# Two stores moved behind the last load, and part of the first x loaded in six-partition transfers, in a batched matmul

## The chip, the cores and the metric

The kernel runs on one core of a Trainium2 chip. The metric is the device time of one execution in microseconds (us). Before the change it was 517.46 us (median of 3 runs, 517.2 to 518.03). Faster or slower needs 2%; kernels were measured in up to five rounds beside runs of the kernel before on the same chip (three chips in all, so compare runs of the same rounds first). A ratio below is the mean time of one kernel's fast runs over that of the other's of the same rounds, so it is not quite the ratio of the quoted medians.

## The reference

```python
batch, m, k, n = 32, 512, 1024, 768
x = randn(batch, m, k)            # float32
weight = randn(batch, k, n)       # float32
out = np.matmul(x, weight)        # float32
```

## The kernel before

Every batch loads 2 MB of x and 3 MB of weights from HBM and stores 1.5 MB. All loads but the first x are issued by GpSimd (POOL) on the *software queue*, which casts float32 to bfloat16 on the way (the page counts 1024 KB for such a load of x, half of what it reads). The first x goes as float32 on SyncE's (SP's) *hardware queue* (2048 KB on the page), and so do the stores of the end. TensorE (PE) transposes x and multiplies; ScalarE and VectorE copy the results out of its accumulators. Loads are issued three to four batches ahead. The last four batches take their weights in pieces.

```python
CHUNKED = {B - 4: (4, 4), B - 3: (4, 4), B - 2: (4, 4), B - 1: (4, 2, 2)}
AHEAD = 3
LATE = 4
# w_pool has 4 buffers, x_pool 5, out_pool 7                      (cut)

x_first = first_pool.tile([P, MT, K], F32)            # 128 x 4 x 1024
nc.sync.dma_start(x_first, x_view[0])                 # hardware queue
load_w(0)                                             # software queue
...
for b in range(B):
    if b + AHEAD + 1 < B:
        load_x(b + AHEAD + 1)                         # software queue
    if b + AHEAD < B:
        load_w(b + AHEAD)                             # software queue
    if 0 < b <= B - LATE:
        nc.gpsimd.dma_start(out=out_view[b - 1], in_=outs[b - 1])
    if b == B - 1:                                    # hardware queue
        # half of out[30], out[28], out[29], the other half of out[30]  (cut)
    ...  # transposes, matmuls, evacuation; out[31] goes in two halves on SP
```

Of the kernel before, what the change touches and what calls it, by code (L numbers as in the profile page):

```python
# [12 lines left out]
@with_exitstack  # L13
def kernel(
    ctx: ExitStack,
    tc: tile.TileContext,
    x: bass.AP,
    weight: bass.AP,
    out: bass.AP,
):  # L20
    nc = tc.nc
    B, M, K = x.shape
    _, _, N = weight.shape
    P = 128
    MT = M // P
    KT = K // P
    JT = KT // 2
    N2 = 2 * N
    CHUNKED = {B - 4: (4, 4), B - 3: (4, 4), B - 2: (4, 4), B - 1: (4, 2, 2)}
    AHEAD = 3  # L30
    LATE = 4

    const = ctx.enter_context(tc.tile_pool(name="const", bufs=1))
    first_pool = ctx.enter_context(tc.tile_pool(name="first", bufs=1))
    w_pool = ctx.enter_context(tc.tile_pool(name="w", bufs=4))
    x_pool = ctx.enter_context(tc.tile_pool(name="x", bufs=5))
    xT_pool = ctx.enter_context(tc.tile_pool(name="xT", bufs=8))
    out_pool = ctx.enter_context(tc.tile_pool(name="out", bufs=7))
    tpsum = ctx.enter_context(tc.tile_pool(name="tpsum", bufs=2, space=bass.MemoryType.PSUM))
    mpsum = ctx.enter_context(tc.tile_pool(name="mpsum", bufs=2, space=bass.MemoryType.PSUM))  # L40



    w_view = weight.rearrange("b (ki ko) n -> b ki ko n", ki=P)
    x_view = x.rearrange("b (mi mo) k -> b mi mo k", mi=P)
    out_view = out.rearrange("b (mi mo) n -> b mi (mo n)", mi=P)

    xs, ws, outs = {}, {}, {}

    def banks():  # L50
        return [mpsum.tile([P, 512], F32, name=f"pm{i}") for i in range(3)]

    def load_x(b):
        xs[b] = x_pool.tile([P, MT, K], BF16, name="x_sb")
        nc.gpsimd.dma_start(out=xs[b], in_=x_view[b])  # L55

    def load_w(b):
        ws[b] = w_pool.tile([P, KT, N], BF16, name="w_sb")
        at = 0
        for n in CHUNKED.get(b, (KT,)):  # L60
            nc.gpsimd.dma_start(out=ws[b][:, at:at + n, :], in_=w_view[b, :, at:at + n, :])  # L61
            at += n

    def transpose(b, mt):

        pt = tpsum.tile([P, JT, P], F32, name="pt")
        pairs = xs[b].bitcast(F32)
        for j in range(JT):
            nc.tensor.transpose(pt[:, j, :], pairs[:, mt, j::JT], ident)  # L69
        xT = xT_pool.tile([P, JT, P, 2], BF16, name="xT")  # L70
        nc.vector.tensor_copy(  # L71
            xT.rearrange("p j m r -> p (j m r)"), pt.bitcast(BF16).rearrange("p j m -> p (j m)")
        )
        return xT

    def transpose_first(mt):

        xT = xT_pool.tile([P, JT, P, 2], BF16, name="xT")
        for h in range(2):
            pt = tpsum.tile([P, JT, P], F32, name="pt")  # L80
            for i in range(JT):
                nc.tensor.transpose(pt[:, i, :], x_first[:, mt, JT * h + i::KT], ident)  # L82
            nc.vector.tensor_copy(  # L83
                xT[:, 2 * h:2 * h + 2].rearrange("p j m r -> p j r m"),
                pt.rearrange("p (j r) m -> p j r m", r=2),
            )
        return xT



    SPLITS = (
        ((0, 0, 0, 512), (1, 0, 512, N - 512)),
        ((1, N - 512, 0, 1024 - N), (2, 0, 1024 - N, N2 - 1024)),
    )

    def matmuls(pm, half, xT, b, kos, together):
        for ko in kos:
            for i, (bank, at, off, size) in enumerate(SPLITS[half]):
                shares = half == 1 and i == 0
                nc.tensor.matmul(  # L100
                    pm[bank][:, at:at + size],
                    xT[:, ko // 2, :, ko % 2],
                    ws[b][:, ko, off:off + size],
                    start=(ko == 0 and not (together and shares)),
                    stop=(ko == KT - 1),
                    skip_group_check=together,
                )

    def evacuate(b, pair, pm):
        o = outs[b][:, pair * N2:(pair + 1) * N2]  # L110
        nc.scalar.copy(o[:, 0:512], pm[0])  # L111
        nc.vector.tensor_copy(o[:, 512:1024], pm[1])  # L112
        nc.scalar.copy(o[:, 1024:N2], pm[2])  # L113

    with tc.manual_schedule():
        x_first = first_pool.tile([P, MT, K], F32)
        nc.sync.dma_start(x_first, x_view[0])
        load_w(0)
        ident = const.tile([P, P], F32)
        make_identity(nc, ident)  # L120
        for b in range(1, AHEAD):
            load_x(b)
            load_w(b)
        load_x(AHEAD)

        for b in range(B):
            if b + AHEAD + 1 < B:
                load_x(b + AHEAD + 1)
            if b + AHEAD < B:
                load_w(b + AHEAD)  # L130
            if 0 < b <= B - LATE:
                nc.gpsimd.dma_start(out=out_view[b - 1], in_=outs[b - 1])  # L132
            if b == B - 1:
                halves = [slice(pair * N2, (pair + 1) * N2) for pair in range(2)]
                nc.sync.dma_start(out_view[b - 1, :, halves[0]], outs[b - 1][:, halves[0]])
                for late in range(B - LATE, B - 2):
                    nc.sync.dma_start(out_view[late], outs[late])
                nc.sync.dma_start(out_view[b - 1, :, halves[1]], outs[b - 1][:, halves[1]])
            outs[b] = out_pool.tile([P, MT * N], F32, name="out_sb")
            if b not in CHUNKED:  # L140
                turn = transpose if b else lambda _, mt: transpose_first(mt)
                xT = {mt: turn(b, mt) for mt in (0, 1)}
                for pair in range(2):
                    pm = banks()
                    for half in range(2):
                        if pair == 0:
                            matmuls(pm, half, xT[half], b, range(KT), False)
                            xT[2 + half] = turn(b, 2 + half)
                        else:
                            matmuls(pm, half, xT[2 + half], b, range(KT), False)  # L150
                    evacuate(b, pair, pm)
                continue
            xT = {0: transpose(b, 0)}
            pms = [banks() for _ in range(2)]
            at = 0
            for n in CHUNKED[b]:
                last = at + n == KT
                for mt in range(MT):
                    if mt + 1 not in xT and mt + 1 < MT:
                        xT[mt + 1] = transpose(b, mt + 1)  # L160
                    matmuls(pms[mt // 2], mt % 2, xT[mt], b, range(at, at + n), True)
                    if last and mt % 2 == 1:
                        pair = mt // 2
                        evacuate(b, pair, pms[pair])
                        if b == B - 1:
                            nc.sync.dma_start(out_view[b, :, halves[pair]], outs[b][:, halves[pair]])
                at += n
# [30 lines left out]
```

## Time and profile before

| | before |
|---|---|
| time, median | 517.46 us |
| span of the profiled run | 515.2 us |
| PE busy | 429.3 us (83%) |
| software queue, share of 16 DMA engines | 96.8% |
| HBM traffic | 167.77 MB read, 50.33 MB written, 423 GB/s |
| last matmul ends | near 507 us |

First the page of the profiled run: the span in 40 slices. A digit is the busy share of a slice in tenths (9 is 90% or more).

```profile
PE   0999898798788888788887899787998787999793
...
DMA  8999999999999999999999999999999999999996
```

The DMA row is full in every slice but the first and the last; PE has gaps. The page's line of the chain of work that ended last, shares by engine:

```profile
DMA 88%; PE 8%; issue 1%; POOL 1%; DVE 0%; ACT 0%; POOLq 0%
```

The page's DMA queues: packets, MB, and the share of 16 engines' span.

```profile
q0 software_dynamic: 13824, 126.88, 96.8%
q1 hardware_dynamic: 1008, 8.39, 4.0%
q8 instruction: 20, 0.33, 0.2%
q14 instruction: 5, 0.04, 0.0%
```

Two of these rows are nothing the program asked for: 20 packets of 16 KB and 5 of 8 KB bring instructions. 0.2% looks like nothing. But the packets lie on single DMA engines. The packet records of the trace (start, duration, queue, size) show it: every engine moves a 12 KB store packet every 0.457 us, and the software queue gives each engine the same packets (each of its 96 transfers ends in 16 semaphore writes, one per engine). Behind each 16 KB instruction packet one engine's packets start about 1.07 us later from then on. So engines drift apart, and in this run nothing brought them together again: the 16 writes of one load span 0.60 us near 15 us and 3.5 us near 405 us.

The end of the span, by the view of stretches. Columns: stretch, length, busy time of PE, its weight loads, VectorE, ScalarE, GpSimd, then PE's clock, the DMA share and GB/s.

```profile
core 0: us, PE busy (x) PEld busy (x) DVE busy (x) ACT busy (x) POOL busy (x), PEclk, DMA share, GB/s
506.00:508.00 2.00, 0.78 (x6) 0.26 (x3) 0.74 (x2) 1.22 (x3) 0.00 (x0) 1.00 0.80 335
508.00:510.00 2.00, 0.00 (x0) 0.00 (x0) 0.00 (x0) 0.00 (x0) 0.00 (x0) 0.85 1.02 421
510.00:512.00 2.00, 0.00 (x0) 0.00 (x0) 0.00 (x0) 0.00 (x0) 0.00 (x0) 0.50 0.60 246
512.00:514.00 2.00, 0.00 (x0) 0.00 (x0) 0.00 (x0) 0.00 (x0) 0.00 (x0) 0.50 0.14 58
```

There is a hole at 506 to 508 us (share 0.80), and from 510 us fewer and fewer engines work. The semaphore writes of the last store, one per DMA engine, say how many finish when (worked out from the packet records; they come out 0.7 to 0.9 us larger than on the zero of the view of stretches, so read their spread, and differences between lists to some 0.2 us):

```
before, last store, 16 writes (us): 511.6 511.6 511.6 511.7 511.8 511.9 512.0 512.0
   512.2 512.3 512.4 512.5 513.6 513.7 514.2 514.2
```

Three waits (engine, line, tile <- what it waited for: us in total, times, longest), and the two ends of PE's last 26 us in the timeline. PE stands 3.38 us, until 480.85, for the weights of batch 30, w(30), and the last matmuls end near 507:

```profile
PE pm L100 <- DMA w_sb<-in_weight_dram: 63.7, 26, 3.7
...
POOL w_sb L61 <- PE pm L100: 35.0, 7, 13.0
...
PE pt L82 <- DMA x_first<-in_x_dram: 12.3, 1, 12.3
```

```profile
480.85 1.55 PE L100 MATMUL pm<-w_sb,xT 128*128 128x512 bf16 x8 [3.38 <-DMA w_sb<-in_weight_dram]
...
498.81 7.96 PE L100 MATMUL pm<-w_sb,xT 128*128 128x512 bf16 x48
```

SP's transfer of the first x in the timeline (start, us, engine, line, count):

```profile
0.74 0.38 SPq L117 DMA_DIRECT2D x_first<-in_x_dram  x1
```

### The profile page before, as it was taken

What the parts mean: (1) busy time and instruction counts of PE and PEld (TensorE: products, weight loads), DVE (VectorE), ACT (ScalarE), POOL (GpSimd) and SP (SyncE); (2) the same over time, 40 slices, a digit from 0 to 9 for tenths busy, and PEclk for the clock granted to TensorE, in tenths of its full rate; (3) what the DMA queues carried; (4) which work ended last, traced back from release to release, by engine and by line L of the source; (5) the groups of instructions that cost most, each with busy time, mean ns of one, the idle gap of its engine ahead of it and who ended that gap; (6) DMA issues with size and microseconds to landing.
All of it is one profiled execution on the core that took longest, in us unless ns stands there. A gap on an engine that the chain in (4) does not pass through costs nothing.

```text
span 515.2 us, 5979 instructions
## 1 busy us (share of the span) xinstructions
PE 429.3 (83%) x2576; PEld 279.5 (54%) x2576; DVE 129.8 (25%) x196; ACT 76.2 (15%) x129; POOL 51.7 (10%) x102
## 2 busy tenths in 40 slices
PE   0999898798788888788887899787998787999793
PEld 0666465465455555455554556454665455665461
DVE  0433232313223313133132232222331223232231
ACT  0011111111011111111111111010111111111011
POOL 3010100011001010100101001100101010111000
PEclk9999899989889989799898999898999889899897
DMA  8999999999999999999999999999999999999996
GB/s 254 219 215 213 218 274 273 254 239 277 276 275 270 234 270 276 273 274 244 253 278 274 275 256 241 275 276 275 266 243 263 275 279 269 247 251 274 274 384 275
DMA packets 14857, 135.64 MB, mean 263 GB/s; under 512 B 1648, under 2 KB 1648, under 8 KB 3312
## 3 DMA queue, kind: packets, MB, share of 16 engines
q0 software_dynamic: 13824, 126.88, 96.8%
q1 hardware_dynamic: 1008, 8.39, 4.0%
q8 instruction: 20, 0.33, 0.2%
q14 instruction: 5, 0.04, 0.0%
HBM read 167.77 MB, written 50.33 MB: 423 GB/s over the span
## 4 chain that ended last, share of the span: by engine, by line
DMA 88%; PE 8%; issue 1%; POOL 1%; DVE 0%; ACT 0%; POOLq 0%
DMA w_sb<-in_weight_dram 40%; DMA out_dram<-out_sb 25%; DMA x_sb<-in_x_dram 23%; PE pm L100 7%; PE pt L69 1%; POOL w_sb L61 0%; POOL x_sb L55 0%; DVE out_sb L112 0%; DVE xT L71 0%; ACT out_sb L113 0%; POOL ident masks.py:199 0%; POOL ident masks.py:197 0%; POOLq L132 0%; POOLq L61 0%; POOLq masks.py:199 0%
## 5 line engine op out<-in xcount | busy, mean ns | idle before, releaser
L100 PE MATMUL pm<-w_sb,xT 128*128 128x256 bf16 (+1 forms) x2048 | 374.5, 342 | 65.2 <-DMA w_sb<-in_weight_dram 63.7
L100 PEld LDWEIGHTS <-xT 128*128 128x128 bf16 x2048 | 207.5, 102 | 207.7 <-issue 72.5
L71 DVE COPY xT<-pt 128x1024 bf16<-128x1024 bf16 x124 | 82.8, 689 | 230.0 <-PE pt L69 230.0
L111 ACT COPY out_sb<-pm 128x512 f32<-128x512 f32 x64 | 37.5, 585 | 293.2 <-PE pm L100 293.2
L112 DVE COPY out_sb<-pm 128x512 f32<-128x512 f32 x64 | 43.9, 687 | 128.1 <-PE pm L100 128.1
L69 PEld LDWEIGHTS pt<-ident,x_sb 128*128 128x128 f32 x496 | 72.6, 207 | 6.3 <-issue 1.0
L69 PE MATMUL pt<-ident,x_sb 128*128 128x128 f32 x496 | 75.1, 285 | 0.0
L113 ACT COPY out_sb<-pm 128x512 f32<-128x512 f32 x64 | 37.5, 586 | 137.3 <-PE pm L100 137.2
L55 POOL DMA_DIRECT2D x_sb<-in_x_dram x31 | 16.4, 532 | 176.8 <-DMA w_sb<-in_weight_dram 151.3
L61 POOL DMA_DIRECT2D w_sb<-in_weight_dram x37 | 19.7, 534 | 126.3 <-DMA out_dram<-out_sb 59.7
L132 POOL DMA_DIRECT2D out_dram<-out_sb x28 | 15.0, 537 | 118.1 <-DMA x_sb<-in_x_dram 56.4
L82 PE MATMUL pt<-ident,x_first 128*128 128x128 f32 x32 | 6.0, 351 | 12.3 <-DMA x_first<-in_x_dram 12.3
L82 PEld LDWEIGHTS pt<-ident,x_first 128*128 128x128 f32 x32 | 5.0, 204 | 12.9 <-issue 12.2
L83 DVE CAST xT<-pt 128x512 bf16<-128x512 f32 x8 | 5.6, 726 | 19.4 <-PE pt L82 19.1
L111 ACT ACT_TABLE_LOAD x1 | 1.3, 1283 | 0.7 <-PEq L182 0.7
masks.py:199 POOL TENSOR_SCALAR_AFFINE_SELECT ident<-ident 128x128 f32<-128x128 f32 x1 | 0.3, 287 | 0.1
masks.py:197 POOL MEMSET ident<- 128x128 f32 x1 | 0.2, 223 | 0.0
L182 POOL MEMSET const-float32-0.0<- 128x1 f32 x1 | 0.1, 98 | 0.2 <-issue 0.2
L182 POOL MEMSET const-bfloat16-1.0<- 128x1 bf16 x1 | 0.1, 101 | 0.0
L182 POOL MEMSET const-uint8-127<- 128x1 uint8 x1 | 0.1, 101 | 0.0
L182 POOL MEMSET const-float32-1.0<- 128x1 f32 x1 | 0.1, 98 | 0.0
## 6 DMA issues: line engine op xcount, KB each, us to landing
w_sb<-in_weight_dram POOLq DMA_DIRECT2D x28, 1536.0 KB, 43.2
out_dram<-out_sb POOLq DMA_DIRECT2D x28, 1536.0 KB, 42.0
x_sb<-in_x_dram POOLq DMA_DIRECT2D x31, 1024.0 KB, 39.6
w_sb<-in_weight_dram POOLq DMA_DIRECT2D x7, 768.0 KB, 31.4
out_dram<-out_sb SPq DMA_DIRECT2D x4, 768.0 KB, 7.6
out_dram<-out_sb SPq DMA_DIRECT2D x2, 1536.0 KB, 13.7
x_first<-in_x_dram SPq DMA_DIRECT2D x1, 2048.0 KB, 11.4
w_sb<-in_weight_dram POOLq DMA_DIRECT2D x2, 384.0 KB, 27.5
```

What stands on the lines that cost most here:

```text
L55: nc.gpsimd.dma_start(out=xs[b], in_=x_view[b])
L61: nc.gpsimd.dma_start(out=ws[b][:, at:at + n, :], in_=w_view[b, :, at:at + n, :])
L69: nc.tensor.transpose(pt[:, j, :], pairs[:, mt, j::JT], ident)
L71: nc.vector.tensor_copy(xT.rearrange("p j m r -> p (j m r)"), pt.bitcast(BF16).rearrange("p j m -> p (j m)"))
L82: nc.tensor.transpose(pt[:, i, :], x_first[:, mt, JT * h + i::KT], ident)
L83: nc.vector.tensor_copy(xT[:, 2 * h:2 * h + 2].rearrange("p j m r -> p j r m"), pt.rearrange("p (j r) m -> p j r m", r=2),)
L100: nc.tensor.matmul(pm[bank][:, at:at + size], xT[:, ko // 2, :, ko % 2], ws[b][:, ko, off:off + size], start=(ko == 0 and not (together an ...
L111: nc.scalar.copy(o[:, 0:512], pm[0])
L112: nc.vector.tensor_copy(o[:, 512:1024], pm[1])
L113: nc.scalar.copy(o[:, 1024:N2], pm[2])
L132: nc.gpsimd.dma_start(out=out_view[b - 1], in_=outs[b - 1])
L182: nc = _bacc.Bacc("TRN2", target_bir_lowering=False, num_devices=1)
```

## The change

The stores of batches 25 and 26 are held until the last load, w(31), is queued, so that x(31), w(30) and w(31) come sooner and PE ends sooner. They then go out with the store of batch 27, which was queued behind w(31) before the change too; so two stores move, though the code holds three. And 96 of the 128 partitions of the last row tile of the first x come in sixteen transfers of six partitions, which moves bytes from most DMA engines to a few.

```diff
+    HELD = 3
     x_first = first_pool.tile([P, MT, K], F32)
-    nc.sync.dma_start(x_first, x_view[0])
+    nc.sync.dma_start(x_first[:, :MT - 1], x_view[0, :, :MT - 1])
+    for block in range(0, 96, 24):
+        for at in range(block, block + 4):
+            few = slice(at, block + 24, 4)
+            nc.sync.dma_start(x_first[few, MT - 1], x_view[0, few, MT - 1])
+    nc.sync.dma_start(x_first[96:, MT - 1], x_view[0, 96:, MT - 1])
...
+    pending = []
     for b in range(B):
...
-        if 0 < b <= B - LATE:
-            nc.gpsimd.dma_start(out=out_view[b - 1], in_=outs[b - 1])
+        if b <= B - LATE:
+            if b > 0:
+                pending.append(b - 1)
+            if b + AHEAD < B - HELD or b == B - LATE:
+                for at in pending:
+                    nc.gpsimd.dma_start(out=out_view[at], in_=outs[at])
+                pending = []
```

## The prediction

> **What bounds the kernel.** DMA. The 40-slice row shows the DMA engines at 90% or more in every slice but the first and last; the chain of waits that ended last is 88% DMA, 8% PE. The packet records show the end: every engine moves packets at the same pace (a 12 KB store packet every 0.457 us, 26.9 GB/s), yet the 16 semaphore writes of the last store do not come together: eight near 511.5 us, four at 511.9-512.5, four at 513.6-514.2, in a span of 515.2.
>
> The cause I read: the instruction queue fetches 20 blocks of 16 KB, one about every 25 us, and each sets one engine back by 1.07 us. By 405 us eight engines lag the other eight by 2.4-3.5 us; the last four fetches give four of these a third delay. The software queue gives each engine the same bytes, so nothing evens this out. Only light engines wait for data (a hole at 506-508 us, 11 of 16 busy). The four late engines are never idle after 3 us: their own bytes set the time.
>
> **What the change does, costed.**
>
> 1. Held stores. The stores of batches 25 and 26 (3.66 us each on the engines) no longer stand before x(31), w(30), w(31). w(30), which PE awaited until 480.85, lands 3.7 us earlier, w(31) about 7.3. PE was done with its earlier work at 477.5, so its end goes from 507 to about 503.5. No byte is removed. The hole closes, but its engines are not the last; for the late four this is worth 0 to 0.2 us. Seven output buffers suffice for the held stores.
>
> 2. The first x. [...] The trace of before has no such transfer and does not number engines. Engines 0-5 take 64 KB for the 24 KB they had: +1.5 us at 26.9 GB/s, plus 0.3 us for 16 semaphore packets of 22 ns. Engines 6-15 lose 24 KB: -0.9 us. If the late four are among 6-15, the end moves up by 0.9 us; light ones have about 4 us of slack once the hole is closed. SP issues 17 more DMAs (0.35-0.7 us each) beside a busy queue. w(0) lands up to 1.5 us later, so PE's matmuls start later; they do not bound.
>
> **On the critical path:** the 0.9 us of part 2.
>
> **Predicted:** 516.5 us (-0.2%), range 515.2 to 517.9. Faster by over 2%: 0.01; within 2%: 0.98; slower by over 2%: 0.01.
>
> **What would show it.** The last w landing 7 us earlier; PE ending near 503.5; no hole at 506-508; the semaphore writes of the last store spread less, the last near 513.3; 20 fetches as before; hardware-queue bytes unchanged; PE's first transpose before 12.3 us, its first matmul later.
>
> **What would make it wrong.** If a late engine is among 0-5, the time rises by 1.5 to 2 us (about 519). If fetches fall on other engines after the change, the tail shifts by 1 us either way. If the main part of x_first ends before the software queue starts (6.4 us), engines 6-15 get a hole. If the late four do wait for data at the end, part 1 is worth up to 1 us.

The forecast's sum came to -0.9 us, all of it from part 2 (517.46 to about 516.5). Read "engines 0-5" as the six that such a transfer loads and "engines 6-15" as the other ten. That they are six, the trace of the changed kernel shows: its sixteen small transfers have 96 row packets of 4 KB in groups of six, and six engines then stand 2.8 to 3.0 us behind the earliest one (below).

## The result, and the profile after

The changed kernel took 517.44 us (median of 6: 517.48, 516.32, 517.53, 516.44, 517.4, 517.48), the kernel before 517.15 (median of 6 by then, 516.99 to 518.03). The ratio is 0.9996, interval 0.9983 to 1.0009: the same. The six times are not spread: they lie on two levels 1.1 us apart, 516.3 to 516.4 and 517.4 to 517.5. The kernel before has no such levels.

The page after, the same rows:

```profile
PE   0039999999999988779879779887898976999990
...
DMA  8999999999999999999999999999999999999996
```

```profile
DMA 63%; PE 30%; DVE 3%; issue 1%; ACT 0%; POOLq 0%
```

```profile
q0 software_dynamic: 13824, 126.88, 96.7%
q1 hardware_dynamic: 1248, 8.39, 4.1%
q8 instruction: 20, 0.33, 0.2%
q14 instruction: 5, 0.04, 0.0%
```

The bytes of each queue and the 20 fetches are as before. The DMA row is as full as before. PE's row is not: it is empty in the first two slices and full from the fourth to the fourteenth, and the chain now has 30% of PE. The waits, and SP's first transfers (start, us from the first to the end of the last, count):

```profile
POOL w_sb L62 <- PE pm L101: 66.2, 8, 35.2
...
PE pm L101 <- DMA w_sb<-in_weight_dram: 43.9, 17, 4.4
...
PE pt L83 <- DMA x_first<-in_x_dram: 33.6, 1, 33.6
```

```profile
0.74 0.39 SPq L119 DMA_DIRECT2D x_first<-in_x_dram  x1
1.19 20.33 SPq L123 DMA_DIRECT2D x_first<-in_x_dram  x16
22.62 0.36 SPq L124 DMA_DIRECT2D x_first<-in_x_dram  x1
```

The sixteen small transfers took SP 20.33 us, not the 8 that I had allowed. The packet records show their pace: on each of the six engines one packet of the software queue stands between a row packet (172 ns) and its semaphore write, and one more before the next row packet, so a transfer takes 1.98 us beside weight packets (0.91 us each) and 1.38 beside x packets (0.61). What held SP itself is not shown. The tile arrived late, and PE's first transpose came at 33.57 us instead of 12.28. GpSimd's wait for PE to free a weight buffer grew from 13.0 to 35.2 us. Yet the DMA engines saw nothing of it, before and after:

```profile
16.00:34.00 18.00, 17.70 (x112) 11.77 (x111) 6.23 (x11) 2.93 (x5) 1.60 (x3) 1.00 1.04 218
34.00:140.00 106.00, 92.51 (x565) 60.36 (x564) 28.17 (x43) 16.39 (x28) 10.61 (x20) 0.95 1.02 252
```

```profile
core 0: us, PE busy (x) PEld busy (x) DVE busy (x) ACT busy (x) POOL busy (x), PEclk, DMA share, GB/s
16.00:34.00 18.00, 0.43 (x2) 0.46 (x3) 0.00 (x0) 0.00 (x0) 0.00 (x0) 1.00 1.04 229
34.00:140.00 106.00, 103.23 (x644) 69.54 (x655) 33.87 (x51) 18.14 (x31) 11.15 (x21) 1.00 1.02 253
```

In the first stretch PE lost 17.3 us of work. In the second it did 10.7 us more than before, with the DMA share at 1.02 in both. The loads queued ahead carried the engines over.

The end of the timeline and of the span, after:

```profile
478.32 1.48 PE L101 MATMUL pm<-w_sb,xT 128*128 128x512 bf16 x8 [0.31 <-DVE xT L72]
...
494.66 7.96 PE L101 MATMUL pm<-w_sb,xT 128*128 128x512 bf16 x47
```

```profile
core 0: us, PE busy (x) PEld busy (x) DVE busy (x) ACT busy (x) POOL busy (x), PEclk, DMA share, GB/s
506.00:508.00 2.00, 0.00 (x0) 0.00 (x0) 0.00 (x0) 0.00 (x0) 0.00 (x0) 0.83 1.00 421
508.00:510.00 2.00, 0.00 (x0) 0.00 (x0) 0.00 (x0) 0.00 (x0) 0.00 (x0) 0.50 0.84 350
510.00:512.00 2.00, 0.00 (x0) 0.00 (x0) 0.00 (x0) 0.00 (x0) 0.00 (x0) 0.50 0.45 187
512.00:514.00 2.00, 0.00 (x0) 0.00 (x0) 0.00 (x0) 0.00 (x0) 0.00 (x0) 0.50 0.07 31
```

PE ends 4 us earlier, near 502.6, and the hole at 506 to 508 us is gone (share 1.00 for 0.80), both as foreseen. The end still isn't earlier. The semaphore writes of the last store tell why:

```
after, last store, 16 writes (us): 511.1 511.4 511.5 511.5 511.6 511.7 511.7 511.9
   511.9 512.0 512.3 512.4 512.7 513.0 513.6 514.9
```

Three of the four late engines have come forward. One has not, and it is alone at the end, 1.3 us behind the next.

The trace also says which one. The next fence gives how far each engine's landing (its semaphore write) lies behind the earliest one, sorted, for one software-queue load at a time; the time is that of the earliest engine. In the load that lands from 49 us on, six engines stand apart: five by 2.8 to 3.0 us, and one by 3.9, because the first instruction fetch (50.6 us) has hit one of the six on the way. The ninth fetch, at 222 us, hits it again, and the seventeenth, at 425 us, a third time. No other 16 KB fetch among the first seventeen hits one of the six.

```
after, landing of w(0), 14.6 us:  0 .10 .29 .41 .45 .50 .51 .55 .56 .62 .63 .69 .71 .73 .77 .86
after, landing of x(4), 49.0 us:  0 .08 .29 .38 .43 .47 .48 .52 .54 .59 | 2.76 2.83 2.87 2.91 3.00 3.94
after, landing at 219.1 us:       0 .29 .53 1.35 1.50 1.55 1.59 1.71 1.80 1.84 2.77 2.83 3.18 3.22 3.66 5.01
```

### The profile page after: what moved, and what is told of

Read it like the earlier page. It is cut to its first block, busy times and chain, and to the rows that moved or that the text cites. A ratio compares the mean times of both kernels' runs of the same rounds, so it can differ in the third digit from the quotient of the medians.

```text
span 515.7 us, 5952 instructions
## 1 busy us (share of the span) xinstructions
PE 417.8 (81%) x2528; PEld 276.1 (54%) x2576; DVE 129.9 (25%) x196; ACT 76.2 (15%) x129; POOL 51.7 (10%) x102
## 4 chain that ended last, share of the span: by engine, by line
DMA 63%; PE 30%; DVE 3%; issue 1%; ACT 0%; POOLq 0%
PE pm L101 27%; DMA w_sb<-in_weight_dram 25%; DMA out_dram<-out_sb 16%; DMA x_sb<-in_x_dram 16%; DMA x_first<-in_x_dram 6%; PE pt L70 2%; DVE out_sb L113 1%; DVE xT L72 1%; PE pt L83 1%; ACT out_sb L114 0%; POOLq L144 0%; POOLq L62 0%; POOLq L56 0%
## 5 line engine op out<-in xcount | busy, mean ns | idle before, releaser
L101 PE MATMUL pm<-w_sb,xT 128*128 128x256 bf16 (+1 forms) x2000 | 363.4, 336 | 51.3 <-DMA w_sb<-in_weight_dram 43.9
L101 PEld LDWEIGHTS <-xT 128*128 128x128 bf16 x2048 | 204.5, 101 | 185.8 <-issue 52.9
```

The lines of the kernel that those rows point to most:

```text
L101: nc.tensor.matmul(pm[bank][:, at:at + size], xT[:, ko // 2, :, ko % 2], ws[b][:, ko, off:off + size], start=(ko == 0 and not (together an ...
```

## The experiments

Theory A: the time is set by the DMA engine with most to move, instruction fetches included. Eight engines fetch, in a fixed cycle, 20 blocks in all, so four of them fetch a third time. (The trace of before: near 405 us the writes of eight engines come 2.44 to 3.52 us after the earliest one, those of the other eight at most 1.29 after it, and the times that the fetch packets take repeat with the ninth, 893, 893, 948, 945, 935, 974, 975, 948, then 893, 893, 949, 945, 935, 975, 974, 961 ns.) One of the eight is among the six that the change loads (hit by the first, the ninth and the seventeenth fetch, above). Theory B: the gain was made but paid back by PE's late start, or the end hangs on PE. Theory C: which engines get the bytes doesn't matter.

| run | ran | median us (all) | ratio to before | 95% interval |
|---|---|---|---|---|
| hold_only | 5 | 517.67 (516.95 to 518.16) | 1.000 | 0.9986 to 1.0014 |
| split_only | 5 | 517.38 (516.34, 516.38, 517.38, 517.57, 517.6) | 0.9992 | 0.9979 to 1.0004 |
| even16 | 5 | 517.5 (517.32 to 517.95) | 1.0001 | 0.9989 to 1.0014 |
| stairs | 1 | 517.59 | - | - |
| five | 5 | 516.23 (516.17 to 516.73) | 0.9976 | 0.9964 to 0.9989 |
| five_more | 5 | 517.61 (517.45 to 517.68) | 1.0001 | 0.9988 to 1.0013 |
| five_more_unheld | 5 | 517.61 (517.37 to 517.72) | 1.000 | 0.9986 to 1.0014 |
| six_double | 4 | 518.66 (517.8, 518.33, 518.99, 519.14) | 1.002 | 1.0006 to 1.0033 |
| change_16 (wrong result) | 5 | 516.35 (516.31 to 516.43) | 0.9985 | 0.9973 to 0.9998 |
| before_16 (wrong result) | 5 | 516.14 (515.92 to 516.29) | 0.998 | 0.9966 to 0.9994 |
| five_unheld | 5 | 516.22 (516.12 to 516.42) | 0.9982 | 0.997 to 0.9995 |

### hold_only: the held stores alone

```diff
-    (all 18 transfers of parts of x_first)
+    nc.sync.dma_start(x_first, x_view[0])
```

> The held stores alone; the first x loaded in one transfer as before. Theory A (the DMA engine with the most bytes sets the time: the engines that fetch instruction blocks are last and never idle, so moving stores changes nothing for them): 517.2 us, ratio 1.000 within 0.001, PE's end about 503.5 us, the hole at 506-508 us gone, the last four semaphore writes still about 2 us after the first eight. Theory B (the chain of loads, PE and last stores sets the end, so PE's earlier end is worth something): 516 us or less.

It took 517.67 us at ratio 1.000: no gain that these runs can tell from nothing (the interval is 0.7 us either way), as A says. PE's last matmuls began at 495.34 instead of 498.81 us, the hole was gone (share 0.97), and the last engine still wrote its semaphore at about 515.4, on the zero of the lists above (the profiled run is the slowest of the five, 518.16). PE's earlier end is real, and no wait of the end hangs on it.

### split_only: the six-partition transfers alone

```diff
-    (held stores)
+    if 0 < b <= B - LATE:
+        nc.gpsimd.dma_start(out=out_view[b - 1], in_=outs[b - 1])
```

> The sixteen six-partition transfers alone, stores in their old order. Theory A: as the whole change, two levels about 1.1 us apart (near 516.4 and 517.5), depending on whether the one fetching engine among the six loaded ones takes three fetches or two in that execution. Theory B (the late start of PE, 33.6 us instead of 12.3, costs what the relief gains, and the held stores give it back): slower than before by 1 us or more, 518.2 us.

Two levels, 516.34 and 516.38, and 517.38 to 517.6. So the levels come from the transfers, and the held stores were not paying for PE's late start, which is as late here as in the change.

### even16: PE late, every engine's bytes as before

```diff
-    (16 transfers of six partitions x one row of 4 KB, one of 32 partitions)
+    for at in range(0, P, 16):
+        for part in (slice(0, K // 2), slice(K // 2, K)):
+            few = slice(at, at + 16)
+            nc.sync.dma_start(x_first[few, MT - 1, part], x_view[0, few, MT - 1, part])
```

> The held stores, and the last row tile of the first x in sixteen transfers over sixteen partitions (half rows of 2 KB), so that PE starts late (25 to 34 us) but every DMA engine has the same bytes as before. Theory A: PE's late start is free while the loads ahead of it last, so the time equals that of the held stores alone, 517.2 us, at one level and not two. Theory B (PE's late start costs time): 518 us or more.

517.5 us, one level, ratio 1.0001: no cost and no gain on balance. (That sixteen partitions load all engines alike is read from the change's transfer over 32 partitions, whose 32 row packets lie two on each of the sixteen engines.) PE's timeline shows how late it was. With blocks of neighbouring partitions it could start on the first row tiles at 10.31 us (with the change's strided partitions its first transpose waited until 33.57), but it still stood until 33.28 us for the last row tile:

```profile
10.31 3.89 PE L83 MATMUL pt<-ident,x_first 128*128 128x128 f32 x16 [10.31 <-DMA x_first<-in_x_dram]
...
33.28 1.94 PE L83 MATMUL pt<-ident,x_first 128*128 128x128 f32 x8 [9.50 <-DMA x_first<-in_x_dram]
```

This is not the full delay of the change (PE got two groups of matmuls done before), so it bounds B rather than kills it; *five* below has a similar delay (36.6 us) and is faster than before.

### stairs: numbering the engines

```diff
-    (16 transfers of six partitions, one of 32)
+    at = 0
+    for n in (*range(15, 1, -1), 9):
+        nc.sync.dma_start(x_first[at:at + n, MT - 1], x_view[0, at:at + n, MT - 1])
+        at += n
```

> A probe, not for speed: the last row tile of the first x goes in transfers over 15, 14, 13 ... 2 and 9 partitions, one row each per engine, so that each engine is marked by how many of them set it back (about 0.17 us each for a 4 KB packet with its semaphore). If the number of partitions is the number of engines [...], the set-backs form a staircase over the engines, and the eight engines that show the 1.07 us jumps of the instruction fetches can be numbered. Theory A expects exactly one of them among engines 0 to 5. A rival (the fetches move to other engines from run to run) would show none or several.

No trace carries the number of a DMA engine. In the change each small transfer shows six row packets, one per engine. In this probe the first three transfers show 15, 14 and 13, and all of them 128. If each set of engines lies inside the one before, the last transfer (over 9) ends nine queues of different length, and it does. The numbers here and below come from this order alone: the lower the number, the smaller the transfers that still use the engine.

```
last row packet of each engine, us: 31.85 31.84 (engines 0, 1)  30.53 (2)  29.20 (3)
   27.92 (4)  27.03 (5)  25.83 25.71 25.62 (6 to 8)   the others earlier
jump after the 1st fetch (39.3 us): 0.88 + 0.21 us, on the engine with its last row at 27.03
jump after the 2nd fetch (60.3 us): 0.88 + 0.20 us, on the engine with its last row at 25.83
```

In this execution the first engine in the cycle of fetches is engine 5, the second one of 6 to 8. Later jumps could not be given to numbered engines for certain, because engines whose packets start within a few ns of one another get confused in the tracking. Which other engines are in the cycle is not shown. That engine 5 is in it and no engine below is what the next run tests.

### five: the same with five partitions

```diff
-    for block in range(0, 96, 24):
-        for at in range(block, block + 4):
-            few = slice(at, block + 24, 4)
-            nc.sync.dma_start(x_first[few, MT - 1], x_view[0, few, MT - 1])
-    nc.sync.dma_start(x_first[96:, MT - 1], x_view[0, 96:, MT - 1])
+    for at in range(0, 80, 5):
+        few = slice(at, at + 5)
+        nc.sync.dma_start(x_first[few, MT - 1], x_view[0, few, MT - 1])
+    nc.sync.dma_start(x_first[80:, MT - 1], x_view[0, 80:, MT - 1])
```

> The whole change, but with sixteen transfers of five partitions (engines 0 to 4 by the probe's staircase) and 48 partitions in the last one, so that engine 5, the first in the cycle of fetches, is relieved as well (-20 KB, 0.75 us) and no loaded engine fetches. Theory A: 516.6 us (0.75 us below before), at one level, with no second level 1.1 us higher. Rival C (which engine fetches doesn't matter, six-partition transfers are worth nothing as such): 517.4, or two levels as with six partitions.

516.23 us, 0.9976 of before, and the level of 517.5 is gone (one run at 516.73). That is 0.4 us better than I expected. One partition less per transfer, that is one engine less, is the difference that was meant. It isn't the only one: the five partitions are neighbours, so that PE's first transposes start at 10.34 us and not at 33.57, and the other engines are relieved of 20 KB and not 24. Neither explains the gain: *even16* has neighbouring partitions and gains nothing, and a smaller relief should gain less. This falsifies C. One thing more differs from the kernel before. The first landings of w(3) and w(4) lie 12.39 us apart in its packet records, near 68 us (12.63 in hold_only, 12.47 in before_16), and 12.14 to 12.15 in *five*, *five_unheld*, the change and *even16*. What delays them there was not tested, nor what it is worth; some 0.25 us of what *five* gains over the kernel before may come from it. The last stretches, to be read beside those of before and after: at 512 to 514 us the share is 0.02 instead of 0.14 and 0.07, and the last semaphore write came at 513.5 instead of 514.2 and 514.9.

```profile
506.00:508.00 2.00, 0.00 (x0) 0.00 (x0) 0.00 (x0) 0.00 (x0) 0.00 (x0) 0.50 1.02 427
508.00:510.00 2.00, 0.00 (x0) 0.00 (x0) 0.00 (x0) 0.00 (x0) 0.00 (x0) 0.50 0.95 396
510.00:512.00 2.00, 0.00 (x0) 0.00 (x0) 0.00 (x0) 0.00 (x0) 0.00 (x0) 0.50 0.52 218
512.00:514.00 2.00, 0.00 (x0) 0.00 (x0) 0.00 (x0) 0.00 (x0) 0.00 (x0) 0.50 0.02 9
```

### five_unheld: five partitions, stores as before

> The sixteen transfers of five partitions (4 KB each) with the stores in the order of before. Theory A: as with the held stores, 516.2 us within 0.3 us, since the hole before the last store ends before the late engines do. Theory B: 0.5 us or more slower than with the held stores.

516.22 us. The edit is the transfers of *five* in the kernel before, with its own order of stores. The held stores are worth nothing here either: PE's last matmuls begin 5.1 us later than in *five* (497.99 for 492.88) and the time is the same, though the two ran in separate rounds; the pair below ran in the same ones.

### five_more and five_more_unheld: more bytes to the first five

```diff
-    (16 transfers of five partitions x 4 KB)
+    cut = MT * K - 1536          # the last 6 KB of a partition's 16 KB
+    (16 transfers of five partitions x 6 KB, the rest of the cut in one)
```

> As the run with five partitions, but 6 KB of each of the 80 partitions instead of 4 KB: every engine but the first five is relieved of 30 KB (1.1 us), the first five get 66 KB more (2.5 us), which they have room for because they fetch nothing. Theory A: 516.2 us, 1.1 us below before, one level. If engines 0 to 4 have less room than I read, they become last and the time is 516.5 to 517.

> The same transfers of five partitions with 6 KB, the stores in the order of before. Theory A: the held stores only close a hole on engines that are not last, so the time is that of the held version within 0.3 us, 516.2 us. Theory B (the end of PE matters for the end): slower than the held version by 0.5 us or more.

Both missed: 517.61 us, 1.4 us above what I expected, though the two agree with one another, as A says of the held stores. Again one engine was alone at the end (514.9 us, the next 513.0), this time one of the loaded five. It started 0.6 us behind the other four, and I had overlooked the second instruction row, the five packets of 8 KB (in the change's trace such a packet set an engine back by 0.3 to 0.65 us). Two of them hit this engine:

```
five_more, the loaded five, us behind the earliest engine
 92 us: 3.91 4.08 4.13 4.14 4.72      124 us, after the 8 KB fetch at 119: ... 5.16
219 us: 3.78 3.95 4.32 4.33 5.12      314 us, after the 8 KB fetch at 294: ... 5.77
```

So engines 0 to 4 are not free of fetches; one of them had two of the small ones here. The room that I computed for them was an average over engines, and it is the worst one that counts.

### six_double: the suspected cost doubled

```diff
-    few rows of MT - 1 (4 KB a partition), sixteen transfers of six partitions
+    few rows of MT - 2 and MT - 1 (8 KB a partition), sixteen transfers of six partitions
```

> The whole change with the suspected cost doubled: each of the sixteen six-partition transfers takes two row tiles, 8 KB a partition, so engine 5 gets 40 KB more again (1.5 us), with the same number of transfers. Theory A: two levels, 1.5 us above those of the change, 519.0 and 517.9. Theory B or C: 517.4 or below, since the others are relieved once more.

518.99, 519.14, 518.33 and 517.8 us: up by about 1.5 us at the upper level (519.0 for 517.5), and again one engine alone at the end, at 516.4 us, the next at 514.9. By its packet records it is a loaded one that the third fetch hit, and the eleventh. One of the four runs lies between the levels. More relief for ten engines made the kernel slower, because one fetching engine is among the six.

### change_16 and before_16: fewer fetches

```diff
-    matmuls(pm, half, xT[half], b, range(KT), False)            # and for the other pair
+    matmuls(pm, half, xT[half], b, range(5 if b < 8 else 6), False)
-    stop=(ko == KT - 1),
+    stop=(ko == (KT - 1 if together else kos[-1])),
```

> Wrong result on purpose: the whole change with 1024 fewer instructions on PE (some matmuls of the first 28 batches left out), so that it should fetch 16 blocks instead of 20, two for each of the eight engines; every data transfer stays. Theory A: one level instead of two, since no engine gets a third fetch in any execution: about 516.4 us, the lower level of the change. A rival that doesn't tie the levels to the fetches keeps two levels, or 517.4.

> Wrong result on purpose: the kernel before with the same 1024 fewer instructions on PE, 16 fetches instead of 20. Theory A: the four engines with a third fetch set its time, so it falls by about one set-back of 1.07 us, to 516.4 us, with no other change. A rival (the fetches are noise beside the data) leaves it at 517.4.

Leaving out 1024 PE instructions makes the result wrong, and every data transfer stays. The page of change_16 counts 16 fetches, as does that of before_16:

```profile
q8 instruction: 16, 0.26, 0.2%
```

So a fetch goes with 1024 / 4 = 256 PE instructions here (the page of before has 5152 matmuls and weight loads on PE for its 20 fetches, 258 each). PE's waits show no cost of the fetches: in the kernel before, the longest in total are for weights (63.7 us) and for the first x (12.3), and the only other one listed is 1.5 us for VectorE. The DMA engine that carries the block does pay: the kernel before became 1.0 us faster (517.13 to 516.14 in these rounds, one set-back), and the changed kernel lost its upper level and stayed at 516.35, because now, with 16 fetches in a cycle of eight, every fetching engine fetches twice (in the profiled one, the loaded engine that fetches was hit by the seventh). Beside before_16 in the same rounds the change gains nothing: 516.31 to 516.43 us for 515.92 to 516.29, so with the third fetches gone its transfers cost some 0.2 us. PE also had less to do in these two runs, but PE's time had no effect in hold_only, five_unheld and even16.

## Why the prediction was right or wrong

The time, 517.44 us, lies in the range (515.2 to 517.9), and "within 2%" was right. That is partly luck: the range is 2.7 us wide, and all but one of the variants tried here have their median in it. The sum was wrong: I gave the change 0.9 us, and it got that in two of six runs.

- **DMA bounds, and the late engines are those that fetch.** Right. Fewer fetches alone made the kernel before 1.0 us faster (before_16).
- **The held stores are worth 0 to 0.2 us.** Nothing contradicts it: ratio 1.000 alone (known to 0.7 us), and 517.61 us with and without them in five_more and five_more_unheld. The details were right too: PE's end at 502.6 (503.5 foreseen), the hole closed.
- **"If the late four are among 6-15, the end moves up by 0.9 us."** This is the step that failed. In the profiled execution, one of the upper level, the four engines with a third fetch were not all among 6 to 15: one of them, engine 5 of *stairs*, was among the six loaded ones. It set the end at 514.9, while the other three came forward to 512.7 to 513.6. I had named the case, but took the other one for the forecast without a ground for it: the trace of before does not number engines.
- **"If a late engine is among 0-5 ... about 519."** The mechanism was right and the size too large: 517.5. The set-back of the loaded six against the other ten was about as computed (0.9 + 1.5 + 0.3 = 2.7 us; the trace shows 2.8 to 3.0 behind the earliest engine, initial offsets included). But I added it to the latest of the late four. Engines also start up to 0.9 us apart, and whether engine 5 was one of the four, and which, the trace of before can't say. How much of the difference this explains stays open.
- **The second level**, at 516.3 to 516.4, I did not foresee. No execution at the lower level was profiled. Where the cycle of fetches begins is not fixed: the one loaded engine that fetches was hit first by fetch 1 in the profiled execution of the change, by fetch 3 in those of split_only and six_double, and by fetch 7 in that of change_16. With 20 fetches in a cycle of eight, an engine whose first is one of the first four gets three, any other two. The reading that fits: 20 fetches are two and a half rounds of eight, so if the cycle goes on from one execution to the next, engine 5 fetches three times in some executions and twice in others, 1.07 us apart. change_16, with two whole rounds, has one level. That the start differs is shown; that the cycle carries over from one execution to the next is my reading of the two levels, not shown.
- **PE's first transpose before 12.3 us.** Wrong: 33.57 us. I took 17 transfers at SP's own cost of issuing them, 0.35 to 0.7 us; they cost 1.27 us each (20.33 / 16); on the engines a software-queue packet of 0.61 or 0.91 us stood between each two of their packets. I also overlooked that the first transposes would wait for all pieces; with neighbouring partitions they don't (10.31 us in even16, 10.34 in five). This was free only because the loads queued ahead last longer: the load of w(4), which waits for PE, went out at 51.1 instead of 29.6 us, and what was queued before it had landed on the earliest engine by 60.2 us, so some 70% of the lead was used, and the DMA share stayed at 1.02.

The best version measured is the plain one: the kernel before with sixteen five-partition transfers (five_unheld, ratio 0.9982, or five with the held stores, 0.9976). It beats the kernel before clear of noise, by about 0.2%, which is within the 2% that counts as the same. Against the change there are only separate rounds: 516.2 us is at or a little below its lower level, and without the upper one.

## What to carry to other kernels

Here the DMA engines were full from beginning to end (share 1.02), and the time was that of the fullest single engine (alone at 514.9 us in the change, 1.3 us behind the next), which averages (a queue at 0.2%, a mean share) hid: look at how the 16 semaphore writes of the last transfer are spread. The number of partitions of a transfer moved bytes between engines (transfers over six loaded six engines and left them 2.8 to 3.0 us behind the earliest), but first find out which engines carry what the program didn't ask for; the relief for ten engines was worth nothing at the change's upper level (517.4 to 517.5 us, 517.15 before), because one of the other six was already last. An earlier end of PE (by 3.5 us in hold_only, ratio 1.000), or a start 21 us late, changed nothing while the queued loads covered it, but here the late start had used up some 70% of that cover.
